# A decoder trunk on one core: first loads by contraction half, transposes between the first products, banks finished in turn, statistics and sums moved later

## The chip, the cores and the metric

The kernel runs on 1 core of one Trainium2 chip. The metric is device time in microseconds (us) of one execution; shorter is better. Every time below is of that core.

## What is computed

A decoder trunk with two layers on 528 tokens (16 learned meta tokens and 512 of the sequence), width 1024, feed-forward width 2816, all in float32:

```python
h = concatenate([meta, x])
for l in range(2):
    h = layer_norm(ALPHA*h + 0.5*swiglu(h, ffn1_wg[l], ffn1_wu[l], ffn1_wd[l]))   # norm 0, norm 3
    mix = short_conv(h) if l == 0 else forgetting_attention(h, k, v, c)
    h = layer_norm(ALPHA*h + mix)                                                 # norm 1, norm 4
    h = layer_norm(ALPHA*h + 0.5*swiglu(h, ffn2_wg[l], ffn2_wu[l], ffn2_wd[l]))   # norm 2, norm 5
    if l == 0:
        k, v, c = shared_kv(h)
return h[:, 16:]
# swiglu(x, wg, wu, wd) = (silu(x @ wg) * (x @ wu)) @ wd
# layer_norm: mean and variance over the 1024 features of each token, then gain and bias
```

The gains, biases and the scalar factor of each norm are as in the reference; the text below speaks of the six norms by the numbers 0 to 5 above.

## The kernel before

Activations lie transposed, features on the partitions and tokens in the columns: `y` is 128 x 8 x 528. The tokens are worked on in two **halves** of 264 columns (256 in layer 1). Every product of two float32 matrices is three matmuls of split operands: a CAST on ScalarE (ACT) gives the high part (`xh`, `wh`), a subtraction on VectorE (DVE) the low part (`xl`, `wl`), and `gemms` (line 244) issues `wl*xh`, `wh*xl`, `wh*xh` for each 128-row slice of the contraction. One such slice of one product is called a **job**. `split_w` (lines 132, 134) splits weights, `split_x` (lines 257, 258) activations. PE's order is the order in which the code is written (a manual schedule); ACT, DVE, the DMA queue of SP and POOL are ordered by a scheduler, which `behind(...)` ties to instructions named to it. `later(n, fn)` calls `fn` after `n` further jobs.

The work is a sequence of stages. In a feed-forward block gate and up products are computed by **units** of 256 columns each of wg and wu. Most units (class `Unit`) use a scheme of seven products p1 to p7 instead of eight, on sums of weight blocks (`Quads.sums`, s1 to s4, lines 200 to 211) and sums of activations (`Mixed.sums`, t1 to t4, lines 326 to 337). The first unit behind a norm (class `Direct`) computes its eight products plainly: half 0, then half 1, each over four PSUM banks (`pc`), first contraction half n=0 for all four, then n=1, then `finish` for both column blocks m (Silu, line 669; product with the up part, line 670; split). Weights come in through `Quads.load` (line 183), one load for each contraction half and matrix.

A norm is spread over the products in front of it. `Norm.add` (lines 409 to 416) sums values and squares as the tiles of `y` are made (line 508). `Norm.post` (line 424) multiplies the sums by a matrix of ones, four matmuls that give mean and mean square of each column; `down` calls it through `later(LAG[h], ...)`, that is 4 jobs behind the last tile of half 0 and 8 jobs behind that of half 1. `Norm.finish` then subtracts (434), forms the inverse root (350 to 358) in a chain on DVE, and for each pair of tiles subtracts and multiplies (444, 445), applies gain and bias on ACT (448) and splits (257, 258). The products of half 0 of the next stage run while half 1 goes through this.

At the very start `x` and `meta` arrive with tokens on the partitions. They are loaded in column halves (lines 706 and 711), transposed by PE (line 729, three transposes for each of eight tiles m and each token half), copied to `y` on ACT (line 733) and split. `turn_x(0)` writes all 24 transposes of half 0 ahead of the first product; the 24 of half 1 stand in one block behind the first 8 jobs.

The last stage, norm 5, transposes back and takes its statistics with `bn_stats` (line 1113), two groups of 512 for each 128 tokens.

Of the kernel before, what the change touches and what calls it, by code (L numbers as in the profile page):

```python
# [9 lines left out]
F32 = mybir.dt.float32  # L10
# [8 lines left out]
P = 128  # L19
# [13 lines left out]
CHUNKS = ((0, 4), (4, 6), (10, 6), (16, 6))  # L33

LEAD = 3
LAG = (4, 8)
SOON = 600
AHEAD = 3

# [7 lines left out]
def trunk_kernel(  # L47
# [59 lines left out]


    newest = []

    @contextmanager
    def behind(*after):
# [7 lines left out]
    def split_w(src, shape, home=None):  # L120

        n = math.prod(shape)
        if home:
            wh, wl = (home(t).rearrange("p k c -> p (k c)")[:, :KD * P] for t in ("wh", "wl"))
        else:
            wh = wp.tile([P, KD * P], F32R, tag="wh", name="wh")
            wl = wp.tile([P, KD * P], F32R, tag="wl", name="wl")
        if len(shape) == 3:
            a, b = (t[:, :n].rearrange("p (j k n) -> p j k n", j=shape[0], k=shape[1]) for t in (wh, wl))
        else:  # L130
            a, b = (t[:, :n].rearrange("p (k n) -> p k n", k=shape[0]) for t in (wh, wl))
        nc.scalar.copy(a, src)  # L132
        with behind(*newest[-1:]):
            nc.vector.tensor_tensor(b, src, a.bitcast(F32), ALU.subtract)  # L134
        return a, b

    class Weights:
# [147 lines left out]
    class Mixed:  # L285
# [26 lines left out]
        def early(self):  # L312
# [2 lines left out]
            self.left("a11")  # L315
            self.left("a12")

        def sums(self):

            b = self.part  # L320
            w = self.w
            new = lambda n: gtile(n, 2 * w).rearrange("p (k c) -> p k c", k=2)
            t = {}
            for k in range(0, KH, 2):
                t1 = new("t1")
                nc.vector.tensor_tensor(t1, b(0, 0, k), b(0, 1, k), ALU.subtract)
                split_x(*self.tiles("t1", k), t1)
            self.left("s1")
            for k in range(0, KH, 2):
                t3, t2 = new("t3"), new("t2")  # L330
                nc.vector.tensor_tensor(t3, b(1, 1, k), b(0, 1, k), ALU.subtract)
                nc.vector.scalar_tensor_tensor(t2, b(0, 0, k), -1.0, t3, ALU.mult, ALU.subtract)
                split_x(*self.tiles("t2", k), t2)
                split_x(*self.tiles("t3", k), t3)
                t[k] = t2
            for k in range(0, KH, 2):
                nc.vector.scalar_tensor_tensor(t[k], t[k], -1.0, b(1, 0, k), ALU.mult, ALU.subtract)
                split_x(*self.tiles("t4", k), t[k])

        def __getitem__(self, name):  # L340
            if name == "b12":
# [242 lines left out]
    class Direct:  # L584
# [6 lines left out]
        def half(self, h, finish):  # L591
            ps = {(j, m): psum(f"pc{j}{m}")[:, :self.w] for m in range(2) for j in range(2)}
            for n in range(2):
                jobs = []
                for m in range(2):
                    wh, wl = self.quads(f"a{m + 1}{n + 1}")
                    jobs += [(ps[j, m], (wh[:, j], wl[:, j]), self.xs[f"b{n + 1}{h + 1}"])
                             for j in range(2)]
                gemms(jobs, range(KH), start=n == 0, stop=n == 1, chained=True)
            for m in range(2):  # L600
                last = finish(m, h, ps[0, m], ps[1, m])
            return last

    def first_four(quads):
# [2 lines left out]
    def run_units(units, finish, direct=None, after=None):  # L607

        if direct:
            xs = units[0].xs
            for h in range(2):
                last = units[0].half(h, direct)
                if h == 0:
                    with behind(*last):
                        xs.sums()
            if after:
                after(0)
        i0 = int(direct is not None)  # L620
        units[i0].p1()
        units[i0].p2()
        for i, u in list(enumerate(units))[i0:]:
            nxt = units[i + 1] if i + 1 < len(units) else None
            u.p5()
            u.p6()
            u.p7()
            if nxt:
                nxt.p1()
            u.p4()  # L630
            u.p3()
            finish(i, u)
            if after:
                after(i)
            if nxt:
                nxt.p2()
# [4 lines left out]
    def ffn(layer, wg, wu, wd, ln, xs, to, last=None, ready=None, ahead=None):  # L641
# [3 lines left out]
        for c, (f0, fn) in enumerate(CHUNKS):  # L645
# [20 lines left out]

            def direct(m, h, pg, pu, split_h=split_h):
                sg = gtile("sg", w)
                nc.scalar.activation(sg, pg, AF.Silu)  # L669
                nc.vector.tensor_tensor(sg, sg, pu, ALU.mult)  # L670
                return split_h(m, h * w, sg)

            units = []
            for i in range(fn // 2):
# [27 lines left out]
    half = D // 2  # L702
    rows = ((0, P), (P, 120), (248, P), (376, P), (504, 8))
    mt = [htile("mt", F32)[:M, :half] for _ in range(2)]
    for j in range(2):
        nc.sync.dma_start(mt[j], meta[:, j * half:(j + 1) * half])
    xt = []
    for i, (r0, n) in enumerate(rows):
        xt.append([htile("xt", F32)[:n, :half] for _ in range(2)])
        for j in range(2):  # L710
            nc.sync.dma_start(xt[-1][j], x[0, r0:r0 + n, j * half:(j + 1) * half])
        if i == 1:
            first.load(0)
    first.load(1)
    vr = gtile("vr", P)[:120]
    nc.gpsimd.dma_start(vr[0:48, :], ln_gain.rearrange("l i (m p) -> (l i m) p", p=P))
    nc.gpsimd.dma_start(vr[48:96, :], ln_bias.rearrange("l i (m p) -> (l i m) p", p=P))
    nc.gpsimd.dma_start(vr[96:120, :], conv_w[0].rearrange("j (m p) -> (j m) p", p=P))
    nc.gpsimd.dma_start(fbias, f_bias.unsqueeze(1))

    def turn_x(h):
        c0, w = SPAN[0][h]
        for m in range(KD):
            ps = psum("pt")
            parts = [(mt, M)] if h == 0 else []
            parts += [(xt[i], rows[i][1]) for i in ((0, 1) if h == 0 else (2, 3, 4))]
            o = 0
            for src, n in parts:
                nc.tensor.transpose(
                    out=ps[:, o:o + n], in_=src[m // KH][:, (m % KH) * P:(m % KH + 1) * P],  # L730
                    identity=ident[:n, :n])
                o += n
            nc.scalar.copy(y[:, m, c0:c0 + w], ps[:, :w])
            if m % 2:
                xs0.made(h, m - 1)
    def turn_vecs():
        ps = psum("pvec")
        nc.tensor.transpose(out=ps[:, :120], in_=vr, identity=ident[:120, :120])
        nc.vector.tensor_copy(vecs, ps[:, :120])

    turn_x(0)
    first_four(first)()
    later(KD, lambda: turn_x(1))
    later(8 * KD, turn_vecs)


# [346 lines left out]
    def last(w, kn, operands):  # L1093

        gain, bias = (
            xtile(n, F32).rearrange("p k c -> p (k c)")[:, :D] for n in ("gain", "bias"))
        nc.gpsimd.dma_start(gain, ln_gain[1, 2:3, :].broadcast_to([P, D]))
        nc.gpsimd.dma_start(bias, ln_bias[1, 2:3, :].broadcast_to([P, D]))
        for h in range(2):
            yv = cols(y, h, 1)  # L1100
            pt = {}
            st = tiny.tile([P, 2, 2, 6], F32, tag="st", name="st")

            def turn(m, yv=yv, pt=pt, st=st):
                g = m // 4
                for t in range(2):
                    if m % 4 == 0:
                        pt[t, g] = psum("pout")
                    nc.tensor.transpose(
                        out=pt[t, g][:, (m % 4) * P:(m % 4 + 1) * P],  # L1110
                        in_=yv[:, m, t * P:(t + 1) * P], identity=ident)
                    if m % 4 == 3:
                        nc.vector.bn_stats(out=st[:, t, g, :], in_=pt[t, g])

            def finish(h=h, pt=pt, st=st):
                mv = tiny.tile([P, 2, 2], F32, tag="mv", name="mv")
                for t in range(2):
                    nc.vector.bn_aggr(out=mv[:, t, :], in_=st[:, t, :, :])
                v, r, a = (tiny.tile([P, 2], F32, tag=n, name=n) for n in "vra")
                nc.vector.tensor_scalar(v, mv[:, :, 1], 4 * EPS, None, ALU.add)  # L1120
                rsqrt(v, r, a)
                for t in range(2):
                    for g in range(2):
                        o = gtile("o", 512)
                        c = slice(g * 512, (g + 1) * 512)
                        nc.vector.scalar_tensor_tensor(
                            o, pt[t, g], mv[:, t, 0:1], gain[:, c], ALU.subtract, ALU.mult)
                        nc.vector.scalar_tensor_tensor(
                            o, o, r[:, t:t + 1], bias[:, c], ALU.mult, ALU.add)
                        r0 = (2 * h + t) * P  # L1130
                        nc.sync.dma_start(out[0, r0:r0 + P, c], o)

            for (m, _), ps in products(
                    [(m, h) for m in range(KD)], w, kn, operands, {}, 1, 0 if h else 3):
                nc.vector.tensor_tensor(yv[:, m, :], yv[:, m, :], ps, ALU.add)
                later(4 + kn * max(0, 3 - m) * h, lambda m=m, turn=turn: turn(m))
            later(KD // 2, finish)
        flush()
# [34 lines left out]
```

## Time and profile before

| | |
|---|---|
| median of 3 runs | 1925.3 us (1923.21 to 1926.7) |
| the profiled execution: its own time | 1922.97 us |
| the profiled execution: span | 1921.2 us |
| mean granted TensorE clock in it | 0.994 |
| PE (matmul) busy | 1878.4 us, 98% of the span |
| DVE busy | 1417.4 us, 74% |
| ACT busy | 875.6 us, 46% |

The profiled execution is 2.3 us below the median. The span runs from the first to the last event that the profiler sees; 1.8 us of the time lie around it. A timeline row gives the start in us from the start of the span, the duration in us, the engine, the line, the operation, out<-in, the shape, and how many like rows were put together; a bracket at its end gives the engine's idle time in front of it and what ended that.

### The profile page before, as it was taken

To read this page: it belongs to the slowest core of one execution; us is meant where nothing else is said; L and a number is where in the kernel's file an instruction comes from. 1 tells how busy PE (TensorE), PEld (TensorE's weight loads), DVE (VectorE), ACT (ScalarE), POOL (GpSimd) and SP (SyncE) were. 2 spreads that over 40 slices of the span, in tenths; PEclk is the share of its full clock that TensorE was granted. 3 is DMA by queue.
4 is the path that set the end of the run, shared out by engine and by line. 5 is a ranking of instruction groups with operands and counts; after the bars stand their busy time and mean duration, and the time that the engine had idled before them with its cause. 6 is when DMAs were issued, how large, how long until landed. Compare 5 with 4: busy or idle time off the path is not lost.

```text
span 1921.2 us, 34484 instructions
## 1 busy us (share of the span) xinstructions
PE 1878.4 (98%) x14467; PEld 1818.5 (95%) x14467; DVE 1417.4 (74%) x2188; ACT 875.6 (46%) x1459; POOL 25.4 (1%) x78
## 2 busy tenths in 40 slices
PE   8999999999999999999999999999999999999997
PEld 7999999999999999999899998989998898989897
DVE  4885858774479776767997887767787787867685
ACT  5353535443245353535454543535455554535360
POOL 0000000000000000000021000000000000000000
PEclk9999999999999999999999999999999999999999
DMA  4333333323330332323224323232523303333241
GB/s 146 100 102 97 101 98 101 98 77 107 103 99 23 121 110 89 110 89 110 88 91 156 111 83 115 83 115 83 182 64 115 99 1 121 98 101 111 90 131 44
DMA packets 180680, 190.41 MB, mean 99 GB/s; under 512 B 5834, under 2 KB 174070, under 8 KB 180526
## 3 DMA queue, kind: packets, MB, share of 16 engines
q1 hardware_dynamic: 178510, 182.74, 29.8%
q0 software_dynamic: 2016, 5.49, 0.8%
q8 instruction: 113, 1.85, 0.4%
q14 instruction: 41, 0.34, 0.1%
HBM read 181.76 MB, written 6.44 MB: 98 GB/s over the span
## 4 chain that ended last, share of the span: by engine, by line
PE 83%; DVE 11%; DMA 3%; ACT 2%; issue 1%; SPq 0%; DVEq 0%; ACTq 0%
PE pb L244 26%; PE pc L244 14%; PE pa L244 6%; PE pcb L244 2%; PE pcv L244 2%; PE pcc L244 2%; PE pq L244 2%; DVE wl L134 2%; DVE xl L258 1%; ACT wh L132 1%; PE psc L977 1%; PE po L1035 1%; DVE y L445 1%; DVE y L508 1%; DVE s L416 1%
## 5 line engine op out<-in xcount | busy, mean ns | idle before, releaser
L132 ACT CAST wh<-raw 128x1024 fp32r<-128x1024 f32 (+1 forms) x440 | 438.6, 1003 | 471.3 <-PE pc L244 73.5
L134 DVE TENSOR_TENSOR wl<-raw,wh 128x1024 fp32r<-128x1024 f32 (+1 forms) x440 | 509.1, 1164 | 189.6 <-ACT wh L132 181.4
L244 PE MATMUL pb<-xh,wl 128*128 128x264 f32 (+1 forms) x1408 | 399.5, 284 | 3.0 <-DVE wl L134 3.0
L244 PE MATMUL pb<-xh,wh 128*128 128x264 f32 (+1 forms) x1408 | 399.7, 284 | 0.0
L244 PE MATMUL pb<-xl,wh 128*128 128x264 f32 (+1 forms) x1408 | 399.3, 284 | 0.0
L244 PE MATMUL pc<-xh,wl 128*128 128x264 f32 (+1 forms) x960 | 275.3, 287 | 6.2 <-ACT sg L669 3.2
L244 PE MATMUL pc<-xl,wh 128*128 128x264 f32 (+1 forms) x960 | 274.4, 286 | 0.5 <-DVE xl L258 0.5
L244 PE MATMUL pc<-xh,wh 128*128 128x264 f32 (+1 forms) x960 | 274.0, 285 | 0.0
L244 PEld LDWEIGHTS pb<-xh,wl 128*128 128x128 f32 x1408 | 265.9, 189 | 3.8 <-issue 3.4
L244 PEld LDWEIGHTS pb<-xh,wh 128*128 128x128 f32 x1408 | 266.0, 189 | 0.0
L244 PEld LDWEIGHTS pb<-xl,wh 128*128 128x128 f32 x1408 | 265.7, 189 | 0.3
L244 PEld LDWEIGHTS pc<-xh,wl 128*128 128x128 f32 x960 | 182.8, 190 | 7.6 <-ACT sg L669 3.7
L244 PEld LDWEIGHTS pc<-xl,wh 128*128 128x128 f32 x960 | 182.8, 190 | 1.0 <-DVE xl L258 0.9
L244 PEld LDWEIGHTS pc<-xh,wh 128*128 128x128 f32 x960 | 183.1, 191 | 0.0
L244 PE MATMUL pa<-xh,wl 128*128 128x264 f32 (+1 forms) x352 | 99.7, 283 | 0.0
L244 PE MATMUL pa<-xh,wh 128*128 128x264 f32 (+1 forms) x352 | 99.7, 283 | 0.0
L244 PE MATMUL pa<-xl,wh 128*128 128x264 f32 (+1 forms) x352 | 99.6, 283 | 0.0
L132 ACT CAST wh<-s 128x1024 fp32r<-128x1024 f32 x44 | 46.1, 1047 | 48.5 <-DVE s L200 12.7
L200 DVE TENSOR_TENSOR s<-raw 128x1024 f32<-128x1024 f32 x44 | 53.7, 1220 | 17.5 <-DMA raw<-in_ffn_wu_dram 16.6
L244 PEld LDWEIGHTS pa<-xh,wh 128*128 128x128 f32 x352 | 66.2, 188 | 0.0
L244 PEld LDWEIGHTS pa<-xh,wl 128*128 128x128 f32 x352 | 66.2, 188 | 0.0
L244 PEld LDWEIGHTS pa<-xl,wh 128*128 128x128 f32 x352 | 66.1, 188 | 0.0
(1920 smaller groups left out, 4458.0 us busy)
## 6 DMA issues: line engine op xcount, KB each, us to landing
raw<-in_ffn_wg_dram SPq DMA_DIRECT2D x88, 512.0 KB, 3.9
raw<-in_ffn_wu_dram SPq DMA_DIRECT2D x88, 512.0 KB, 4.8
raw<-in_ffn_wd_dram SPq DMA_DIRECT2D x48, 768.0 KB, 4.6
raw<-in_conv_w_in_dram SPq DMA_DIRECT2D x12, 1024.0 KB, 4.9
raw<-in_ffn_wd_dram SPq DMA_DIRECT2D x16, 512.0 KB, 3.6
raw<-in_kv_w_dram SPq DMA_DIRECT2D x16, 512.0 KB, 4.8
raw<-in_conv_w_out_dram SPq DMA_DIRECT2D x4, 1024.0 KB, 5.3
raw<-in_attn_w_q_dram SPq DMA_DIRECT2D x4, 1024.0 KB, 4.8
```

Of the source, the lines that this page charges most:

```text
L132: nc.scalar.copy(a, src)
L134: nc.vector.tensor_tensor(b, src, a.bitcast(F32), ALU.subtract)
L200: nc.vector.tensor_tensor(s, a21, a22, ALU.add)
L244: nc.tensor.matmul(ps, lhsT=a[:, k, :], rhs=b(k), start=start and k == ks[0] and j == 0, stop=stop and k == ks[-1] and j == 2, skip_group_ ...
L258: return a, nc.vector.tensor_tensor(dst_l, src32, dst_h.bitcast(F32), ALU.subtract)
L416: self.last[h] = nc.vector.tensor_tensor(self.s2[h], self.s2[h], sq, ALU.add)
L445: nc.vector.tensor_tensor(ym, ym, rb, ALU.mult)
L508: norm.add(h, m, lambda ym=ym, ps=ps: nc.vector.tensor_tensor(ym, ym, ps, ALU.add))
L977: nc.tensor.matmul(ps, lhsT=q[:, M + t * P:M + (t + 1) * P], rhs=kt[:, a:b], start=True, stop=True)
L1035: nc.tensor.matmul(po[:, q0:S], lhsT=vt[:, j * P:(j + 1) * P], rhs=pT[j // 2][:, j % 2, q0:S], start=j == 0, stop=False)
```

## The change

1. SP's queue: the first column halves of `meta` and of the first two blocks of `x`, then the first contraction half of the first weights, then the second halves of each, then the rest of `x`.
2. PE: only the first four tiles' transposes of half 0 stand ahead of the first product; the other four groups come behind jobs 4, 6, 8 and 10, and the eight groups of half 1 behind jobs 12, 14, ... 26.
3. `Direct.half`: in the second contraction half the products run job by job, and `finish(m)` follows each column block's pair of banks.
4. `LAG` goes from (4, 8) to (8, 16) jobs: the four statistics matmuls of norms 0 to 4 come 4 jobs (12 matmuls) later for half 0 and 8 jobs (24 matmuls) later for half 1.
5. `Mixed.sums` is cut in three: t1 as before; t2 and t3 (`more`) ordered behind the Silu of the first column block of half 1; t4 (`fourth`) behind a split of weights.
6. `last`: `bn_stats` on four groups of 256 in place of two of 512 for each 128 tokens.

```diff
-LAG = (4, 8)
+LAG = (8, 16)
...
     class Mixed:
         def sums(self):
             for k in range(0, KH, 2):
                 t1 = self.new("t1")
                 nc.vector.tensor_tensor(t1, b(0, 0, k), b(0, 1, k), ALU.subtract)
                 split_x(*self.tiles("t1", k), t1)
             self.left("s1")
+        def more(self):
             for k in range(0, KH, 2):
...
+        def fourth(self):
+            for k, t in self.t.items():
+                nc.vector.scalar_tensor_tensor(t, t, -1.0, self.part(1, 0, k), ALU.mult, ALU.subtract)
+                split_x(*self.tiles("t4", k), t)
...
     class Direct:
-                gemms(jobs, range(KH), start=n == 0, stop=n == 1, chained=True)
-            for m in range(2):
-                last = finish(m, h, ps[0, m], ps[1, m])
+                if n == 0:
+                    gemms(jobs, range(KH), stop=False, chained=True)
+                    continue
+                for m in range(2):
+                    for job in jobs[2 * m:2 * m + 2]:
+                        gemms([job], range(KH), start=False, chained=True)
+                    last = finish(m, h, ps[0, m], ps[1, m])
...
     def run_units(units, finish, direct=None, after=None):
-            for h in range(2):
-                last = units[0].half(h, direct)
-                if h == 0:
-                    with behind(*last):
-                        xs.sums()
+            with behind(*units[0].half(0, direct)):
+                xs.sums()
+            with behind(units[0].half(1, direct)[0]):
+                xs.more()
...
-            if nxt:
-                nxt.p1()
-            u.p4()
-            u.p3()
+            with behind(*(recent if direct and i == i0 else ())):
+                if direct and i == i0:
+                    xs.fourth()
+                if nxt:
+                    nxt.p1()
+                u.p4()
+                u.p3()
...
             def direct(m, h, pg, pu, split_h=split_h):
-                nc.scalar.activation(sg, pg, AF.Silu)
+                silu = nc.scalar.activation(sg, pg, AF.Silu)
-                return split_h(m, h * w, sg)
+                return silu, *split_h(m, h * w, sg)
...
     for j in range(2):
         nc.sync.dma_start(mt[j], meta[:, j * half:(j + 1) * half])
+        for i in range(2):
+            load_x(i, j)
+        first.load(j)
+    for j in range(2):
+        for i in range(2, 5):
+            load_x(i, j)
...
-    turn_x(0)
+    for m in range(KH):
+        turn_x(0, m)
     first_four(first)()
-    later(KD, lambda: turn_x(1))
+    for h in range(2):
+        for m in range(KH * (1 - h), KD):
+            later(2 * m + 16 * h - 4, lambda h=h, m=m: turn_x(h, m))
...
-                    if m % 4 == 3:
-                        nc.vector.bn_stats(out=st[:, t, g, :], in_=pt[t, g])
+                    if m % 2:
+                        nc.vector.bn_stats(
+                            out=st[:, t, m // 2, :], in_=pt[t, g][:, (m % 4 - 1) * P:(m % 4 + 1) * P])
```

Two places show how it moves instructions. The first is the start of SP's queue (`mt`: meta tokens, `xt`: blocks of `x`, `raw`: weights; the lines are those of each kernel). Before:

```order
L706 DMA mt<-in_meta_dram 16x512 x2
L711 DMA xt<-in_x_dram 128x512 x2
L711 DMA xt<-in_x_dram 120x512 x2
L183 DMA raw<-in_ffn_wg_dram 128x4x256
L183 DMA raw<-in_ffn_wu_dram 128x4x256
L711 DMA xt<-in_x_dram 128x512 x4
```

With the change:

```order
L726 DMA mt<-in_meta_dram 16x512
L723 DMA xt<-in_x_dram 128x512
L723 DMA xt<-in_x_dram 120x512
L184 DMA raw<-in_ffn_wg_dram 128x4x256
L184 DMA raw<-in_ffn_wu_dram 128x4x256
L726 DMA mt<-in_meta_dram 16x512
L723 DMA xt<-in_x_dram 128x512
L723 DMA xt<-in_x_dram 120x512
L184 DMA raw<-in_ffn_wg_dram 128x4x256
L184 DMA raw<-in_ffn_wu_dram 128x4x256
L723 DMA xt<-in_x_dram 128x512 x2
```

The first weights have three loads ahead of them in place of six, and the second contraction half of the weights stands ahead of the last six blocks of `x`.

The second place is ACT's queue at the second half of norm 1, behind the statistics matmuls `pd` (L433 or L441 squares the mean, L448 or L456 applies gain and bias, `xh<-y` is the split's cast, `sg<-pc` the Silu of the first direct unit's half 0 for its two column blocks). Before:

```order
L433 ACTIVATE v<-pd 128x264
L448 ACTIVATE y<-y,vecs 128x264 x3
L257 CAST xh<-y 128x528
L448 ACTIVATE y<-y,vecs 128x264
L669 ACTIVATE sg<-pc_6571 128x264
L257 CAST xh<-y 128x528
L448 ACTIVATE y<-y,vecs 128x264 x3
L257 CAST xh<-y 128x528
L448 ACTIVATE y<-y,vecs 128x264
L257 CAST hh<-sg 128x264
L257 CAST xh<-y 128x528
L669 ACTIVATE sg<-pc_6573 128x264
```

With the change:

```order
L441 ACTIVATE v<-pd 128x264
L683 ACTIVATE sg<-pc_6571 128x264
L683 ACTIVATE sg<-pc_6573 128x264
L456 ACTIVATE y<-y,vecs 128x264 x3
L258 CAST xh<-y 128x528
L456 ACTIVATE y<-y,vecs 128x264 x2
```

Both Silus of half 0 now stand ahead of the first gain-and-bias instruction of half 1; before, the first stood behind four of them and the second behind all eight. At norm 4 the order moves in the same way.

## Rows read from the trace of the kernel before

**Rows 1.** The page, head and busy time.

```profile
span 1921.2 us, 34484 instructions
PE 1878.4 (98%) x14467; PEld 1818.5 (95%) x14467; DVE 1417.4 (74%) x2188; ACT 875.6 (46%) x1459; POOL 25.4 (1%) x78
```

**Rows 2.** Waits of PE: waited for, us in total, times, longest.

```profile
PE pd L424 <- DVE y L508: 9.8, 6, 2.3
```

**Rows 3.** Timeline of PE, from the first transposes to the first products.

```profile
7.25 0.46 PE L729 MATMUL pt<-ident,xt 120*128 120x120 f32 x1 [2.46 <-DMA xt<-in_x_dram]
...
8.46 0.28 PE L729 MATMUL pt<-ident,mt 16*128 16x16 f32 x1
...
9.28 0.28 PE L729 MATMUL pt<-ident,mt 16*128 16x16 f32 x1
...
16.21 0.56 PE L244 MATMUL pc<-xh,wl 128*128 128x264 f32 x1 [2.76 <-DVE wl L134]
...
22.06 2.05 PE L729 MATMUL pt<-ident,xt 128*128 128x128 f32 x11
```

**Rows 4.** Chain of waits, first load of weights.

```profile
3.51 5.62 DMA raw<-in_ffn_wg_dram
```

**Rows 5.** Timeline of ACT and DVE, the first split of weights.

```profile
13.76 1.05 ACT L132 CAST wh<-raw 128x1024 fp32r<-128x1024 f32 x1
14.84 1.23 DVE L134 TENSOR_TENSOR wl<-raw,wh 128x1024 fp32r<-128x1024 f32 x1 [0.53 <-DMA raw<-in_ffn_wg_dram]
```

**Rows 6.** Timeline of PE, holes behind the start.

```profile
56.99 0.36 PE L244 MATMUL pb<-xh,wl 128*128 128x264 f32 x1 [1.14 <-DVE wl L134]
...
74.31 0.39 PE L244 MATMUL pd__783<-hl,wh 128*128 128x264 f32 x1 [0.84 <-DVE hl L258]
...
391.73 0.71 PE L424 MATMUL pd<-y,ones_all 128*128 128x264 f32 x2 [2.25 <-DVE y L508]
...
618.88 0.36 PE L244 MATMUL pb<-xh,wl 128*128 128x264 f32 x1 [1.90 <-DVE wl L134]
...
635.11 0.40 PE L244 MATMUL pd__7119<-hl,wh 128*128 128x264 f32 x1 [0.95 <-DVE hl L258]
...
952.58 0.71 PE L424 MATMUL pd<-y,ones_all 128*128 128x264 f32 x2 [2.19 <-DVE y L508]
...
964.29 0.39 PE L244 MATMUL pc<-xl,wh 128*128 128x264 f32 x1 [0.53 <-DVE xl L258]
...
1404.81 1.22 PE L424 MATMUL pd<-y,ones_all 128*128 128x256 f32 x2 [2.27 <-DVE y L508]
...
1586.15 0.58 PE L244 MATMUL pc<-xh,wl 128*128 128x256 f32 x1 [3.19 <-ACT sg L669]
```

**Rows 7.** Stretches behind four holes: us, busy PE, PEld, DVE, ACT, POOL; PEclk; DMA share; GB/s.

```profile
618.88:623.04 4.16, 4.16 (x21) 4.16 (x22) 3.38 (x4) 0.80 (x2) 0.00 (x0) 0.59 0.56 173
1404.81:1408.20 3.39, 3.39 (x9) 2.76 (x9) 2.44 (x4) 0.78 (x3) 0.00 (x0) 0.52 0.10 21
1586.15:1592.30 6.15, 6.15 (x29) 6.15 (x30) 4.82 (x11) 2.86 (x7) 0.00 (x0) 0.50 0.00 0
392.00:396.00 4.00, 4.00 (x28) 3.74 (x28) 4.00 (x8) 0.52 (x2) 0.00 (x0) 1.00 0.27 81
```

**Rows 8.** Timeline, second half of norm 1: statistics, gain and bias, first split, first product.

```profile
582.48 0.61 PE L424 MATMUL pd<-y,ones_all 128*128 128x264 f32 x2
...
590.02 1.61 ACT L448 ACTIVATE y<-y,vecs 128x264 f32<-128x264 f32 x3 [6.07 <-DVE y L445]
...
592.37 0.70 DVE L258 TENSOR_TENSOR xl<-y,xh 128x528 fp32r<-128x528 f32 x1
...
593.05 0.29 PE L244 MATMUL pc<-xh,wl 128*128 128x264 f32 x1
```

**Rows 9.** Timeline of DVE, first half of norm 0 and the last statistics.

```profile
385.42 0.70 DVE L258 TENSOR_TENSOR xl<-y,xh 128x528 fp32r<-128x528 f32 x1
...
1909.76 1.30 DVE L1113 BATCH_NORM_STATS2 st<-pout 128x6 f32<-128x512 f32 x2 [0.42 <-PE pout L1109]
```

More of the change, by code (lines that the diff above doesn't have):

```diff
@@ L109, in trunk_kernel @@
     newest = []
+    recent = []
     @contextmanager
@@ L131, in split_w @@
             a, b = (t[:, :n].rearrange("p (k n) -> p k n", k=shape[0]) for t in (wh, wl))
-        nc.scalar.copy(a, src)
+        recent[:] = [nc.scalar.copy(a, src)]
         with behind(*newest[-1:]):
-            nc.vector.tensor_tensor(b, src, a.bitcast(F32), ALU.subtract)
+            recent.append(nc.vector.tensor_tensor(b, src, a.bitcast(F32), ALU.subtract))
         return a, b
@@ L316, in early, with new @@
             self.left("a12")
+        def new(self, name):
+            return gtile(name, 2 * self.w).rearrange("p (k c) -> p k c", k=2)
         def sums(self):
             b = self.part
-            w = self.w
-            new = lambda n: gtile(n, 2 * w).rearrange("p (k c) -> p k c", k=2)
-            t = {}
             for k in range(0, KH, 2):
-                t1 = new("t1")
+                t1 = self.new("t1")
                 nc.vector.tensor_tensor(t1, b(0, 0, k), b(0, 1, k), ALU.subtract)
@@ L328, in sums @@
             self.left("s1")
+        def more(self):
+            b = self.part
+            self.t = {}
             for k in range(0, KH, 2):
-                t3, t2 = new("t3"), new("t2")
+                t3, t2 = self.new("t3"), self.new("t2")
                 nc.vector.tensor_tensor(t3, b(1, 1, k), b(0, 1, k), ALU.subtract)
@@ L334, in sums @@
                 split_x(*self.tiles("t3", k), t3)
[L335 to L338, printed above, removed]
+                self.t[k] = t2
+        def fourth(self):
+            for k, t in self.t.items():
+                nc.vector.scalar_tensor_tensor(t, t, -1.0, self.part(1, 0, k), ALU.mult, ALU.subtract)
+                split_x(*self.tiles("t4", k), t)
         def __getitem__(self, name):
@@ L704, in trunk_kernel, with load_x @@
     mt = [htile("mt", F32)[:M, :half] for _ in range(2)]
+    xt = [[htile("xt", F32)[:n, :half] for _ in range(2)] for _, n in rows]
+    def load_x(i, j):
+        r0, n = rows[i]
+        nc.sync.dma_start(xt[i][j], x[0, r0:r0 + n, j * half:(j + 1) * half])
     for j in range(2):
         nc.sync.dma_start(mt[j], meta[:, j * half:(j + 1) * half])
[L707 to L714, printed above, removed]
+        for i in range(2):
[4 more added lines that the diff above has]
+            load_x(i, j)
     vr = gtile("vr", P)[:120]
@@ L719, in trunk_kernel, with turn_x @@
     nc.gpsimd.dma_start(fbias, f_bias.unsqueeze(1))
-    def turn_x(h):
+    def turn_x(h, m):
         c0, w = SPAN[0][h]
[L723 to L735, printed above, removed]
+        ps = psum("pt")
+        parts = [(mt, M)] if h == 0 else []
+        parts += [(xt[i], rows[i][1]) for i in ((0, 1) if h == 0 else (2, 3, 4))]
+        o = 0
+        for src, n in parts:
+            nc.tensor.transpose(
+                out=ps[:, o:o + n], in_=src[m // KH][:, (m % KH) * P:(m % KH + 1) * P],
+                identity=ident[:n, :n])
+            o += n
+        nc.scalar.copy(y[:, m, c0:c0 + w], ps[:, :w])
+        if m % 2:
+            xs0.made(h, m - 1)
     def turn_vecs():
@@ L1101, in last @@
             pt = {}
-            st = tiny.tile([P, 2, 2, 6], F32, tag="st", name="st")
+            st = tiny.tile([P, 2, 4, 6], F32, tag="st", name="st")
             def turn(m, yv=yv, pt=pt, st=st):
@@ L1111, in turn @@
                         in_=yv[:, m, t * P:(t + 1) * P], identity=ident)
-                    if m % 4 == 3:
-                        nc.vector.bn_stats(out=st[:, t, g, :], in_=pt[t, g])
+                    if m % 2:
+                        nc.vector.bn_stats(
+                            out=st[:, t, m // 2, :], in_=pt[t, g][:, (m % 4 - 1) * P:(m % 4 + 1) * P])
             def finish(h=h, pt=pt, st=st):
```

## The prediction

> **What bounds it now.** I read the page's head first: PE is busy 1878.4 us of a span of 1921.2 [rows 1]. The change adds no matmul and removes none, so it can win only the 43 us in which PE stands idle, and the stretches in which it runs at a lower clock. The second view is the list of PE's waits: the statistics matmuls (line 424) wait six times for the last tile, 9.8 us in all [rows 2]; the rest is the start and single holes. The third view, PE's timeline, places these [rows 3, 6]; the fourth, the clock by stretch, shows that behind three holes the granted clock was 0.50 to 0.59, the level of 1.2 GHz [rows 7]. Last I read ACT's and DVE's queues at a norm [rows 8], since the change moves work on those.
>
> **The start.** Before, PE transposes from 7.25, one tile's three in 0.82 us, and its first product starts at 16.21 [rows 3]. Between them stand eight tiles (6.6 us), then ACT's cast of the first weights at 13.76, held in ACT's queue by the copies of those tiles, and DVE's low part from 14.84, 1.23 us [rows 5]. Now four tiles come first (3.3 us less). The first weights were issued at 3.51 and took 5.62 us [rows 4]; with three loads ahead in place of six, some 0.5 MB and three issues less, they land about 1.4 us earlier, and the `x` blocks some 1.3 us earlier (5.9 for 7.25). Transposes then end near 9.2, cast and low part near 11.6, and the first product follows there: 4.6 us sooner. The twelve transposes are not gone. They run between the products and cost 3.3 us at the slow pace of [rows 3], about 1.6 us at full clock. The products from 16.21 to 22.06 took 5.85 us for 24, or 0.24 us each, against a mean of 0.130 over the kernel [rows 1, 3]; I let that slow stretch keep its length. Half 0 of the first unit then ends 2.5 to 3 us sooner. The t4 sums, now behind a weight split, no longer delay the low part that p6 waits for: 1.14 us, and 0.84 us at the first down product goes too, as its activations are ready with time to spare [rows 6]. Together **5.2 us**, with bounds of 1 (all moved transposes at the slow pace, loads no earlier) and 7.
>
> The transposes at 7.25 to 13.5 did not bring the products behind them to full speed: these began slow all the same [rows 3]. The Trainium skill, page "TensorE: Matmul & The Clock Gate", section "Part 4: PE-mode transpose", says that transposes do not count as PE work for the clock as matmuls do. This speaks against mixing them with the first products: if the clock rose later by their 3.3 us, half of that, 1.65 us, would be lost, and the start would be worth 3.6 us.
>
> **Norm 0.** In half 0 the statistics come 12 matmuls later. Its waits go, but the next products then wait for the first split, which ended at 386.12 [rows 9] when PE came to them some 0.3 us later: 0.4 us is all that is won. In half 1 the hole of 2.25 [rows 6] goes, with 24 matmuls (24 x 0.12 = 2.9 us) in it, and the second half's split stays ready in time, as the conv's products of half 0 are many. Together **2.7**, bounds 0.4 and 4.
>
> **Norm 1.** Before, statistics at 582.48, ACT's first gain and bias at 590.02, first split finished at 593.07, and PE comes to half 1 at 593.05 [rows 8]: no slack. Now the statistics stand 2.9 us later, and both Silus stand ahead of the gain and bias. The second Silu can start only when PE has ended half 0, at about 593.1. It takes about 0.36 us; from the first gain and bias to the end of the split are 3.05 us (590.02 to 593.07). So the split ends at 596.4: **a new hole of 3.3 us**. Against it the hole of 1.90 at 618.88 goes, since t4 is out of the way of the weight split, with the slow stretch behind it (21 matmuls in 4.16 us, 0.198 each, 1.4 us more than at the mean), and the 0.95 us at 635.11 [rows 6, 7]. What is queued behind the Silus on ACT is the gain and bias of all eight tiles, and for these DVE's splits and PE wait. Net **+0.9**.
>
> **Norm 2.** The 2.19 and 0.53 us [rows 6] go, but the second half's first split ended at 964.2, and with the same DVE work ahead of it it stays there: the two holes become one of about 3.5 us in front of half 1. Only the 0.3 to 0.4 us of half 0 is won: **+0.4**.
>
> **Norm 3.** The 2.27 us go, and the slow stretch (3.39 us at a clock of 0.52, 1.6 us) [rows 6, 7]. Five heads' products cover the chain nearly; I take 1.1 us of new wait and 0.2 in half 0: **+2.6**.
>
> **Norm 4.** As norm 1, a new hole of 3.3 us ahead of half 1. The hole of 3.19 us at 1586.15 [rows 6], where PE waited for a bank that the Silu of half 1 had to free, goes, since that Silu now stands ahead of the sums; with it the slow stretch: 29 matmuls in 6.15 us, 0.212 each, 2.4 us over the mean [rows 7]. Net **+2.3**.
>
> **The end.** DVE's last two statistics groups took 1.30 us [rows 9]; half of each is now done earlier: **+0.5**.
>
> **New slow stretches.** The three new holes (norms 1, 2, 4) are as long as or longer than any in the middle before. Behind 3.19, 1.90 and 2.27 us the clock fell, behind 2.25 us it did not [rows 6, 7]. The cost of such a stretch, from the three that there are, is 2.4, 1.4 and 1.6 us, mean 1.8; bounds for all three together 0 and 7.2 (three at 2.4). I take three at 1.8: **-5.4**.
>
> **The sum:** 5.2 + 2.7 + 0.9 + 0.4 + 2.6 + 2.3 + 0.5 = 14.6, less 5.4: 9.2 us. From the profiled execution's 1922.97 us that is 1913.8. That execution lies 2.3 us below the median of the runs; by the median, 1925.3, I forecast **1916.1 us**.
>
> **Rivals.**
> - *No slow stretch behind the new holes*: 1916.1 - 5.4 = 1910.7. For it: the hole of 2.25 us without one. Against: the longest hole had the longest. Chance 0.2.
> - *The start gives nothing, and the holes are deep*: loads interleave and the first weights land as before, so that only 1 us is won (4.2 less), and the slow stretches cost 2.4 each (1.8 less): 1922.1, within the bound of no change. For it: the two loads of weights and the tail of `x` share the same engines. Against: half the bytes stand ahead of them. Chance 0.12.
> - *The first clock rise comes late* by the transposes among the products: 1.65 us, 1917.8. It was worked out above; by that rule of the Trainium skill it would be so. Chance 0.15; it stays near the forecast.
> - *Later statistics starve PE at all five norms*: the place is PE between half 0 and half 1, the price per norm a hole of 3.3 us and 2.4 us of slow clock, 5.7. It decides if the products left behind the statistics of half 1 are shorter than the chain of 10.6 us from statistics to first split (582.48 to 593.07 [rows 8]). Norms 0 and 3 then lose 5.7 each where I took 0.3 and 1.1 (10 more), and ACT, held by Silus behind that, keeps the holes at 618.88, 635.11 and 1586.15 with their slow stretches (6.0 + 3.8 = 9.8 more): 1936. Against it: at norms 0 and 3 more products lie there than at the others. Chance 0.06.
> - *The change does nothing to the waits* (the scheduler gives back the old order) is excluded by the order above.
>
> **The numbers.** The forecast as worked out has 0.47, no slow stretch 0.2, late rise 0.15, start and holes 0.12, starved 0.06. The range leaves out the starved case and the upper part of the third: 1908.5 (no slow stretch, start at 7) to 1922. About 0.2%, 3.9 us, is what a measurement of this kernel can tell from no change: faster is below 1921.4, slower above 1929.2. All of the first three cases but a small part of each are faster: 0.8; same 0.14; slower 0.06.
>
> **What would show it.** In the profile after: first product near 11.6; no wait of line 424's matmuls for `y`; no hole near 618 and 1586; the start's first 36 down products done near 69 for 74; new holes of PE in front of the second half behind norms 1, 2 and 4, of 3.3, 3.5 and 3.3 us, with a clock of about 0.5 behind each; none of more than 1.5 us at norms 0 and 3. It is wrong if the first product starts later than 14, if PE's idle time does not fall by some 5 us, or if slow stretches stand at other places.

## The result, and the profile after

The changed kernel takes 1913.2 us (median of 4 runs, 1912.77 to 1913.92) for 1925.3 before: a ratio of 0.9938, 95% interval 0.9921 to 0.9956. The forecast was 1916.1, range 1908.5 to 1922.0. The time lies 2.9 us from the forecast, but the parts behind it do not lie where the sum put them. Every ratio is to the kernel before, run again beside the run in question; its medians there were 1926.0 (e1 to e4), 1927.5 (e5 to e7) and 1924.7 us (e8 to e11), so times of different sets are best compared by ratio.

The head of the page after, as in [rows 1]:

```profile
span 1911.7 us, 34484 instructions
PE 1874.8 (98%) x14467; PEld 1814.6 (95%) x14467; DVE 1416.8 (74%) x2196; ACT 877.1 (46%) x1459; POOL 25.4 (1%) x78
```

The span fell by 9.5 us: 3.6 us are busy time of the same 14467 matmuls (less of it at the low clock), 5.9 us are idle time of PE. The waits of PE after, the largest (waited for, us in all, times, longest); those of line 424, 9.8 us in [rows 2], stand no longer among them:

```profile
PE pc L245 <- ACT xh L258: 6.0, 3, 2.2
PE pc L245 <- DVE wl L135: 5.4, 1, 5.4
...
PE pc L245 <- DVE xl L259: 2.1, 4, 0.5
PE pd__7119 L245 <- ACT hh L258: 1.8, 1, 1.8
```

A hole is a stretch in which PE stands idle, a slow stretch one in which its granted clock is 0.50. The three holes for `xh` are new. PE's timeline shows where they stand, as forecast in front of half 1 behind norms 1, 2 and 4, each with a second small one for `xl`, and a further wait at 631, for the split activations `hh` of the down product:

```profile
591.74 0.39 PE L245 MATMUL pc<-xh,wl 128*128 128x264 f32 x1 [2.04 <-ACT xh L258]
592.67 0.39 PE L245 MATMUL pc<-xl,wh 128*128 128x264 f32 x1 [0.54 <-DVE xl L259]
...
631.03 0.39 PE L245 MATMUL pd__7119<-hh,wl 128*128 128x264 f32 x1 [1.78 <-ACT hh L258]
...
960.51 0.39 PE L245 MATMUL pc<-xh,wl 128*128 128x264 f32 x1 [1.84 <-ACT xh L258]
...
1561.09 0.39 PE L245 MATMUL pc<-xh,wl 128*128 128x256 f32 x1 [2.16 <-ACT xh L258]
```

The holes at 391, 618 and 1586 of [rows 6] are gone. The clock behind the four places (columns as in [rows 7]):

```profile
592.00:596.00 4.00, 3.46 (x28) 3.33 (x28) 3.30 (x6) 4.00 (x9) 0.00 (x0) 1.00 0.02 4
631.00:635.00 4.00, 3.61 (x17) 3.41 (x18) 3.28 (x6) 1.47 (x2) 0.00 (x0) 0.64 1.05 353
961.00:965.00 4.00, 3.57 (x29) 3.57 (x30) 3.61 (x7) 4.00 (x9) 0.00 (x0) 1.00 0.01 4
1562.00:1566.00 4.00, 4.00 (x34) 4.00 (x35) 3.16 (x6) 3.68 (x9) 0.00 (x0) 1.00 0.00 0
```

Behind none of the three new holes did the clock fall in this execution; it fell behind the wait at 631, to a mean of 0.64.

To see where time comes from I set the start of each down stage in one trace against the same one before. The lead gained from stage to stage, in us, for the change and all runs told of below (start: up to the last down stage ahead of norm 0; norm 0 and norm 3: up to the output product behind that norm; norms 1, 2 and 4: up to a down stage of the feed-forward block behind that norm, the second for norm 1 and the first for the others; end: from there to the end of the span; the cells hold to about 0.1 us):

| run | start | norm 0 | norm 1 | norm 2 | norm 3 | norm 4 | end | span won |
|---|---|---|---|---|---|---|---|---|
| the change | 0.7 | 2.7 | -1.8 | 1.2 | 3.8 | 3.6 | -0.7 | 9.5 |
| forecast, slow stretches included | 5.2 | 2.7 | -0.9 | -1.4 | 2.6 | 0.5 | 0.5 | 9.2 |
| e9_change_again | 1.3 | 2.2 | -3.4 | -0.3 | 3.8 | 2.0 | -0.7 | 4.8 |
| e1_lag_back | 1.8 | -1.7 | 4.4 | 0.2 | 0.2 | 5.8 | -0.7 | 10.0 |
| e2_start_back | 0.7 | 2.1 | -1.6 | 1.2 | 3.6 | 3.5 | -0.7 | 8.8 |
| e3_bn_back | 0.7 | 2.3 | -1.7 | -0.9 | 3.8 | 2.2 | -0.1 | 6.3 |
| e11_bn_back_again | 1.5 | 2.5 | -1.9 | -0.5 | 1.5 | 2.0 | -0.1 | 5.1 |
| e4_sums_back | -3.1 | 2.5 | -1.2 | 1.0 | 3.1 | -0.7 | -0.5 | 1.0 |
| e10_sums_alone | 1.1 | 0.4 | 5.1 | -1.6 | 0.7 | 5.7 | -0.2 | 11.2 |
| e6_loads_held | 2.5 | 2.4 | -2.7 | 1.2 | 3.9 | 3.8 | -0.7 | 10.4 |
| e7_transposes_first | -0.1 | 2.4 | -2.1 | -0.6 | 3.6 | 2.1 | -0.6 | 4.8 |
| e5_lag_by_norm | 3.4 | 1.9 | 4.4 | -0.4 | 1.9 | 5.7 | -0.8 | 16.0 |
| e8_best | 2.2 | 2.6 | 3.8 | 1.1 | 3.8 | 5.7 | -0.1 | 19.1 |

### The profile page after: what moved, and what is told of

The parts are those of the page before. It is cut to its first block, busy times and chain, and to the rows that moved or that the text cites. A ratio compares the mean times of both kernels' runs of the same rounds, so it can differ in the third digit from the quotient of the medians.

```text
span 1911.7 us, 34484 instructions
## 1 busy us (share of the span) xinstructions
PE 1874.8 (98%) x14467; PEld 1814.6 (95%) x14467; DVE 1416.8 (74%) x2196; ACT 877.1 (46%) x1459; POOL 25.4 (1%) x78
## 4 chain that ended last, share of the span: by engine, by line
PE 88%; DVE 8%; DMA 2%; ACT 1%; issue 1%; SPq 0%; DVEq 0%; ACTq 0%
PE pb L245 26%; PE pc L245 15%; PE pa L245 6%; PE pcc L245 2%; PE pcv L245 2%; PE pcb L245 2%; PE pq L245 2%; DVE wl L135 1%; PE psc L998 1%; PE po L1056 1%; DVE xl L259 1%; ACT wh L133 1%; DMA raw<-in_attn_w_q_dram 1%; DVE y L453 1%; DVE y L452 1%
## 5 line engine op out<-in xcount | busy, mean ns | idle before, releaser
L245 PE MATMUL pc<-xh,wl 128*128 128x264 f32 (+1 forms) x960 | 275.4, 287 | 11.5 <-ACT xh L258 6.0
```

The costliest lines, as they stand in the source:

```text
L245: nc.tensor.matmul(ps, lhsT=a[:, k, :], rhs=b(k), start=start and k == ks[0] and j == 0, stop=stop and k == ks[-1] and j == 2, skip_group_ ...
```

## The experiments

**One part undone: the places of the statistics.**

```diff
-LAG = (8, 16)
+LAG = (4, 8)
```

> The changed kernel with LAG at (4, 8) again, all else of the change kept. Theory (the later statistics are worth their waits at norms 0, 2 and 3 and cost a hole at norms 1 and 4): the waits of the statistics matmuls for y come back, some 9 us of them, and the holes of 2.6 us in front of half 1 at norms 1 and 4 go; together 2 to 4 us slower than the changed kernel's 1913.2, so 1915 to 1917. Rival (the gain of 9.5 us in the profile comes from the sums and the direct unit's order): no change, 1912 to 1914. Rival of the prediction (the later statistics starve PE): faster by over 2 us.

Measured: 1912.6 us (1909.9 to 1914.1), ratio 0.9930 (0.9915 to 0.9945), as fast as the change: the total is that of the first rival. The theory is right about the places and wrong about the sum. Norms 0, 2 and 3 lose 4.4, 1.0 and 3.6 us against the change, and norms 1 and 4 win 6.2 and 2.2: -9.0 and +8.4. Some of both is chance: a slow stretch followed the returned waits at 391 and 1401, and the one at 632 stayed away. So `LAG` as a whole is worth nothing that these runs can tell, by two effects of about the same size.

**One part undone: the start.** The loads and the transposes of the kernel before, in the changed kernel (the "-" side of the change at SP's queue and at `turn_x`, not all of it printed above).

> The changed kernel with the loads in their old order and the transposes in their old blocks. Theory (the first weights land no earlier, as the loads run side by side, and the transposes among the products eat the earlier first product): the end of the first unit moves by under 0.5 us, and the time by under 1 us: 1912 to 1914.2. The prediction's term (the start is worth 2.5 to 3 us up to the end of the first unit's half 0): 1915.7 or more.

Measured: 1914.3 us (1913.3 to 1918.8), start 0.7 as with the change: theory, 0.1 us above its range. The first product came at 16.67 us instead of 13.46, and the first unit still ended 0.2 us sooner (the first `pb` product at 47.01 for 47.24).

**One part undone: the statistics of the end.**

```diff
-            st = tiny.tile([P, 2, 4, 6], F32, tag="st", name="st")
+            st = tiny.tile([P, 2, 2, 6], F32, tag="st", name="st")
...
-                    if m % 2:
-                        nc.vector.bn_stats(
-                            out=st[:, t, m // 2, :], in_=pt[t, g][:, (m % 4 - 1) * P:(m % 4 + 1) * P])
+                    if m % 4 == 3:
+                        nc.vector.bn_stats(out=st[:, t, g, :], in_=pt[t, g])
```

> The changed kernel with bn_stats on two groups of 512. Theory (the finer groups make PE's transposes wait for DVE at the first four tiles of the second half, 1.1 us, and save 0.5 us at the end): 0.6 us faster, 1912.6, and no wait of pout for st. Prediction's term (0.5 us saved): 0.5 us slower, 1913.7.

Measured: 1917.0 us (1915.6 to 1918.8), neither of the two. The end itself behaved as the theory said, -0.1 for -0.7 us, and the wait of `pout` (the bank that PE transposes into at the end) for `st` (its statistics) is gone. But up to norm 1 the traces run alike, and then norms 2 and 4 lost 2.1 and 1.3 us, at places that this edit does not touch: the granted clock was 0.50 in the middle of slow stretches at 964 and 1564. This called for the repeats further down.

**One part undone: the direct unit's order and the cut sums.** `Direct.half`, `Mixed.sums` and `run_units` as before, the rest as changed.

> The changed kernel with the direct unit's banks finished together and the sums in one piece, as before; loads, transposes, LAG and bn_stats as changed. Theory (the holes at the first unit's p6 and at the Silu of the second half go by this part alone, and at norm 1 what is won is given back at the down product): at norm 4 the hole of 3.2 us and its slow stretch come back (5 us or more), at norm 1 the hole near 618 comes back and the wait of 1.8 us near 631 goes, the p6 wait of the first stage (1.1 us) comes back: 1917 to 1921. Rival (LAG moves the Silus and so removes the holes): under 2 us slower.

Measured: 1924.0 us (1917.5 to 1926.9, 10 runs), ratio 0.9992 (0.9980 to 1.0004): without this part nothing is left of the gain; that is 3 us above the theory's range. The start alone lost 3.8 us against the change, with a slow stretch behind the first hole below (0.50 from 58.85), which is chance again. The holes for `wl` are back. The one at the Silu of half 1 is not, against the theory; in its place there are now holes on either side of it:

```profile
57.84 0.36 PE L245 MATMUL pb<-xh,wl 128*128 128x264 f32 x1 [1.79 <-DVE wl L135]
...
621.41 0.36 PE L245 MATMUL pb<-xh,wl 128*128 128x264 f32 x1 [1.38 <-DVE wl L135]
...
1567.06 0.38 PE L245 MATMUL pc<-xl,wh 128*128 128x256 f32 x1 [1.42 <-DVE xl L259]
...
1593.34 0.36 PE L245 MATMUL pb<-xh,wl 128*128 128x256 f32 x1 [1.50 <-DVE wl L135]
```

(In the code `more` stands behind the Silu of the second column block of half 1, `half(1, direct)[0]` being what the last `finish` returns; item 5 of the change names the first.)

**The same part alone, on the kernel before.**

> The kernel before with the direct unit's order and the cut sums alone; loads, transposes, LAG and bn_stats as before. Theory (this part carries nearly all of the gain: the holes at p6 of the first stage, near 618 and near 1586 with their slow stretches, and the Silus out of the way): 9 to 13 us faster than before, 1912 to 1917. Rival (it needs the later statistics to work): under 5 us faster.

Measured: 1911.8 us (1909.9 to 1913.4), ratio 0.9929 (0.9915 to 0.9944): theory. Together with e4 this is the main finding: this part alone gives all that the whole change gives. It wins 5.1 us at norm 1 and 5.7 at norm 4: the holes of 1.90, 0.95 and 3.19 us [rows 6] are gone, and no new one stands in front of half 1 but 0.57 us for `xl` at 1560.69. How much the order of finish wins, and how much the cut sums, was not tried apart. The waits for `y` stay as they were, and cost a slow stretch by chance (0.56 from 946 to 950):

```profile
PE pd L432 <- DVE y L516: 9.8, 6, 2.3
```

**The place of the statistics by norm.**

```diff
-                    later(LAG[h], lambda h=h: norm.post(h))
+                    later((4, 8)[h] if norm.i in (1, 4) else LAG[h], lambda h=h: norm.post(h))
```

> The changed kernel with LAG (4, 8) at norms 1 and 4 and (8, 16) at norms 0, 2 and 3. Theory (at norms 1 and 4 no statistics matmul waited before, so the later place gives nothing there and costs the hole in front of half 1): the two holes of 2.6 us go; at norm 4 that is kept, at norm 1 a part of it may be lost again at the down product, whose weights come no sooner: 2.5 to 5 us faster than the changed kernel, 1908 to 1910.7. Rival (the earlier statistics bring back the late Silu or another hole of the same length): 1912 to 1914.

Measured: 1906.8 us (1905.8 to 1908.7), ratio 0.9894 (0.9875 to 0.9913): theory, 1.2 us below its range. The start gave 2.7 us more than with the change, which this edit does not touch; norms 1 and 4, which it does, gave 6.2 and 2.1 more. Both holes for `xh` at norms 1 and 4 are gone, and the wait at 631 too (0.75 us for `hl` is left). How that wait had come is seen in DVE's queue at the end of the first `Unit` behind norm 1. In the change the low part of the down weights stands ahead of the gate's product L678, and waits for a cast that waits for its load:

```profile
627.39 1.05 ACT L133 CAST wh<-raw 128x1024 fp32r<-128x1024 f32 x1 [1.63 <-DMA raw<-in_ffn_wd_dram]
...
628.47 1.23 DVE L135 TENSOR_TENSOR wl<-raw,wh 128x1024 fp32r<-128x1024 f32 x1 [1.66 <-ACT wh L133]
629.62 0.70 DVE L678 TENSOR_TENSOR g<-g,u 128x528 f32<-128x528 f32 x1
```

With the earlier statistics at this norm the scheduler put them the other way round:

```profile
621.75 0.70 DVE L678 TENSOR_TENSOR g<-g,u 128x528 f32<-128x528 f32 x1
623.41 1.23 DVE L135 TENSOR_TENSOR wl<-raw,wh 128x1024 fp32r<-128x1024 f32 x1 [0.96 <-ACT wh L133]
```

e1 and e10, with the earlier statistics too, have no wait for `hh` there either. That this order, and not the later PE, makes the wait was not tried by itself.

**The first weights without company.** A one-column copy into each later tile makes its load wait (excerpt):

```diff
+            for t in (mt[1], xt[0][1], xt[1][1], *(xt[i][j] for j in range(2) for i in range(2, 5))):
+                held.append(nc.vector.tensor_copy(t[:, 0:1], y[:t.shape[0], 0, 0:1]))
```

> The changed kernel with a one-column copy by DVE into each tile of the second lot of loads, so that these are issued only when the first tile of y is there (near 5.7 us); 10 tiny copies are added, whose columns the loads overwrite. Theory (the first weights landed at 11.1 as before because the later loads share the engines with them): they land at 8 to 9, the first product starts 2 to 3 us sooner than 13.46, and the end is 1.5 to 3 us sooner, 1910.2 to 1911.7. Rival (512 KB loads take their 8 us from issue whatever runs beside them): first product at 13.4, no change. Second rival (the later loads now hold up the second contraction half): first product sooner, but the wait comes back behind the first 16 jobs.

Measured: 1914.3 us (1912.3 to 1918.4), no change. The later loads were issued from 6.14 us on instead of 3.15, and the first weights still landed at 11.0, where ACT's cast begins:

```profile
11.00 1.04 ACT L133 CAST wh<-raw 128x1024 fp32r<-128x1024 f32 x1 [2.60 <-DMA raw<-in_ffn_wu_dram]
...
13.35 0.59 PE L250 MATMUL pc<-xh,wl 128*128 128x264 f32 x1 [5.37 <-DVE wl L135]
17.34 0.28 PE L250 MATMUL pc<-xl,wh 128*128 128x264 f32 x1
```

So 3 us less of company did not bring them sooner, and the theory that the later loads hold them up is not borne out; between 6.14 and 11.0 they still ran beside them. What sets the landing is open; in runs with the same code as the change the landing lay between 9.74 (e5) and 11.10. Start 2.5 comes from elsewhere: full speed was reached 4.0 us after the first product instead of about 8.

**All transposes of half 0 in front.**

```diff
-    for m in range(KH):
+    for m in range(KD):
         turn_x(0, m)
```

> The changed kernel with all 24 transposes of half 0 ahead of the first product; the 24 of half 1 stay between the products. Theory (the weights bind the first product, so eight tiles fit in front of them for nothing, and the products then pass the slow stretch without transposes in between): first product at 13.5 to 13.9, full speed after 24 products, some 2 us sooner than at 21.1, end 1.5 to 2.5 us faster, 1910.7 to 1911.7. Rival (ACT's copies of the four added tiles delay the weight splits by 2 to 3 us, as before): no change or slower.

Measured: 1920.4 us (1916.4 to 1921.3), ratio 0.9961 (0.9945 to 0.9977): the rival, no gain. First product at 17.65, since the copies of the four added tiles wait for `x` (PE stood 1.32, 0.93 and 0.80 us for its parts) and stand ahead of the weight casts on ACT. But the start lost only 0.8 us against the change's first trace and 1.4 against its repeat; 3.3 us more of the difference to the first trace lie at norms 2 and 4, where slow stretches came as they do in the repeat without this edit. So the transposes are better off among the products by about 1 us in these traces, and the rest of the 7 us between the medians is not shown to come from this edit.

**The change itself again.**

> The changed kernel itself, once more, on the chip that runs the others of this set. Theory (whether a slow stretch follows a hole of 2 us is a matter of the execution and not of the program): the holes and waits stand where they stood to 0.3 us, but the slow stretches, and the first rise of the clock, may stand elsewhere; median 1911 to 1918. Rival (the slow stretches belong to the program): the one slow stretch at 632 and the rise near 21.1 as before, median 1912.7 to 1914.

Measured: 1916.2 us (1913.4 to 1918.2), ratio 0.9948 (0.9931 to 0.9965): theory. The holes stand where they stood (2.04, 2.07, 1.86 and 2.16 us at 591.68, 632.65, 962.13 and 1564.23), but now a slow stretch follows every one of them:

```profile
592.00:596.00 4.00, 3.46 (x17) 3.39 (x17) 3.27 (x6) 4.00 (x10) 0.00 (x0) 0.57 0.00 0
633.00:637.00 4.00, 3.64 (x18) 3.61 (x18) 3.10 (x6) 1.28 (x2) 0.00 (x0) 0.57 0.99 345
963.00:967.00 4.00, 3.94 (x22) 3.94 (x23) 3.62 (x7) 4.00 (x11) 0.00 (x0) 0.67 0.03 6
1564.50:1568.50 4.00, 3.51 (x17) 3.39 (x17) 3.21 (x6) 4.00 (x10) 0.00 (x0) 0.58 0.00 0
```

In the four microseconds from 592 PE did 17 matmuls where it did 28 in the first trace. The same program has one slow stretch in one execution and four in another, and spans of 1911.7 and 1916.4 us. Norms 1, 2 and 4 differ between the two by 1.6, 1.5 and 1.6 us: that is about a slow stretch's price here.

**The old statistics of the end again.**

> e3_bn_back once more, beside the changed kernel on the same chip. Theory (its 1917.0 came from slow stretches by chance behind the holes of norms 2 and 4, not from bn_stats): within 3 us of e9_change_again on either side, and in the profile 0.5 us less than it between the last down products and the end. Rival (bn_stats on two groups is slower by 3 to 4 us): 3 to 4 us over e9_change_again again, with the slow stretches at norms 2 and 4.

Measured: 1915.0 us (1914.8 to 1917.9), 1.2 us under the change beside it: theory. The end took 0.1 us more than before, with the change 0.7 more, in both pairs of traces. At norm 3 this trace gained 1.5 us where the change gained 3.8: PE waited 1.51 us for `first` at 1371.32 and 0.77 us for `wl` at 1382.49, waits that the change's two traces do not have; e5 has the like (1.16 and 0.77). Why was not looked into.

**The parts that win, together** (e5 and e3's edits).

> LAG (4, 8) at norms 1 and 4, (8, 16) at norms 0, 2 and 3, and bn_stats on two groups of 512; all else as changed. Theory (the two parts add up: no hole in front of half 1 at norms 1 and 4, no wait of pout for st): 0.5 us under e5_lag_by_norm's 1906.8, so 1904 to 1909 with slow stretches that come or stay away by chance; no wait of pout for st in the profile. Rival (bn_back as a whole costs 3 us, as e3_bn_back's 1917.0 against 1913.2 would have it): 1909.5 or more.

Measured: 1904.7 us (1903.8 to 1905.9), ratio 0.9894 (0.9879 to 0.9908): in the theory's range. This beats both kernels: 20 us faster than before beside it, 8.5 to 11.5 faster than the change. By ratio it is no faster than e5, so what the old statistics of the end add shows in the stage alone (-0.1 for -0.8). No slow stretch was seen in its trace ahead of the last down stage's end.

## Why the prediction held, and where it did not

The time was in the range and near the forecast because errors of both signs met: the start, norm 1 and the end gave 6.6 us less than forecast, norms 2, 3 and 4 gave 6.9 more. That they cancel is luck. One part of the mechanism was right throughout: the terms that the prediction gives to the cut sums and the order of finish (1.14 and 0.84 at the start, 1.90, 1.4 and 0.95 at norm 1, 3.19 and 2.4 at norm 4, the slow stretches of before among them) make 11.8 us, and e10, which has this part alone, won 11.9 at these three places. By its own steps:

- *The start, 5.2 us.* Measured 0.7 in the profile and 1.3 in the repeat: the step that failed. Its own parts add up to 4.5 to 5.0 and not to 5.2. Two of its terms were wrong. The first is "they land about 1.4 us earlier". It goes by the load of `wg` alone, which landed at 9.13 [rows 4]; the split takes columns of `wg` and `wu`, and `wu` came later. Before, it was issued at 3.95 and took 7.2 us:

```profile
L183 SPq DMA_DIRECT2D raw<-in_ffn_wu_dram x1: 507/507/507, 4.0 to 4.0; - x1
...
DMA to landing us min/median/max: 7.2/7.2/7.2
```

  With the change it was issued at 2.60 and took 8.42 us (row of the chain of waits), and released ACT's cast:

```profile
2.60 8.42 DMA raw<-in_ffn_wu_dram
...
11.10 1.04 ACT L133 CAST wh<-raw 128x1024 fp32r<-128x1024 f32 x1 [2.66 <-DMA raw<-in_ffn_wu_dram]
```

  So the weights were there at 11.0 for 11.2, and the first product came at 13.46 and not at 11.6. (This trace is the latest of the eight with the new start, e6 and e7 left out: that cast began at 9.74 to 11.10, mean 10.5.) The second is "I let that slow stretch keep its length": it grew from 5.85 to about 7.7 us (13.46 to 21.1), with the transposes in it:

```profile
13.46 0.59 PE L245 MATMUL pc<-xh,wl 128*128 128x264 f32 x1 [5.44 <-DVE wl L135]
...
20.79 0.42 PE L245 MATMUL pc<-xh,wh 128*128 128x264 f32 x1
21.14 0.23 PE L746 MATMUL pt<-ident,mt 16*128 16x16 f32 x1
...
21.83 0.28 PE L245 MATMUL pc<-xh,wh 128*128 128x264 f32 x1
```

  This is the mechanism of the rival of the late rise, in this trace at about half the size given there: 24 products ran at the low clock before and 24 now, with two groups of transposes among them and a third at the rise. The Trainium skill's page "TensorE: Matmul & The Clock Gate", section "Part 4: PE-mode transpose", would have it so, and this pair of traces agrees. The other traces do not settle it: with the same code the slow stretch lasted 4.05 us in e5, where the first full-speed product is at 16.14 and the first product at 12.09, and 6.2 us in e1. Over those eight traces the first unit ended at 44.18 to 47.24, mean 46.3; over the three with the old one at 46.66 to 47.01, mean 46.85. So the loads and the transposes are worth some 0.5 us by these means, with 3 us of chance, where 2.5 to 3 were forecast. The holes at p6 and at the first down product (1.14 and 0.84 us) went or shrank as said, by the cut sums: in e4 they are back, in e10 they are not.
- *Norm 0, 2.7 us.* Measured 2.7; and it goes when `LAG` goes back.
- *Norm 1, 0.9 less a slow stretch.* The new hole was forecast at 3.3 (its own terms make 3.4) and is 2.6 us in two pieces. The holes at 618 and its slow stretch went as said. But "the 0.95 us at 635.11" did not go: it became 1.78 and 0.35 us, and there the slow stretch came. Net -1.8 for a forecast of -0.9: sign right, cause half missed.
- *Norm 2, 0.4 less a slow stretch.* Measured 1.2: the first split came about 1.2 us sooner than I let it, so the one hole is 1.84 and 0.54 us and not 3.5 (which is not worked out there: the terms beside it make 3.1).
- *Norm 3, 2.6.* Measured 3.8: the new wait is 0.5 us and not 1.1; the slow stretch at 1404 went too.
- *Norm 4, 2.3 less a slow stretch.* Measured 3.6, the hole 2.65 in two pieces for 3.3, and no slow stretch this time.
- *The end, 0.5 us won.* Measured 0.7 lost, and 0.5 to 0.8 in all traces with the finer groups, for 0.1 to 0.2 without. DVE's last statistics did shrink from the 1.30 us of [rows 9] to 0.76. But PE's transposes of the first four tiles now wait for DVE's statistics of the bank that they write to, and more is given away there than is won at the end: 0.6 us at the second half, whose rows these are, and 0.5 at the first (near 1869). With two groups (e3, e8) neither place loses:

```profile
1891.26 0.88 PE L1130 MATMUL pout<-ident,y 128*128 128x128 f32 x4 [0.44 <-DVE st L1134]
...
1900.77 0.76 DVE L1134 BATCH_NORM_STATS2 st<-pout 128x6 f32<-128x256 f32 x2 [0.42 <-PE pout L1130]
```

- *The slow stretches, 5.4 us.* None of the three came in the profiled execution, all three in the repeat. The mean price of 1.8 us was about right (1.5 to 1.6 measured); that it is certain was wrong. The rows of before could have told: the prediction names one hole of about 2 us without a slow stretch, at 391, but behind the 2.19 us at 952 [rows 6] the clock stayed up too (columns as in [rows 7]):

```profile
952.58:956.60 4.02, 4.02 (x26) 3.76 (x27) 4.02 (x7) 0.79 (x3) 0.00 (x0) 1.00 0.00 0
```

  *The rival of no slow stretch* (1910.7, chance 0.2) describes the first trace at norms 1, 2 and 4 better than the forecast does.
- *The rival of starved norms* fell: norms 0 and 3 have holes of 1.3 and 0.5 us. But its mechanism is there on a smaller scale, at norms 1 and 4, and costs all that the later statistics win at the others.
- *The range and the signs.* The lower end by its own terms is 1910.7 - 1.8 = 1908.9 and not 1908.5. Of the signs, the waits of the statistics matmuls for `y` and the holes near 618 and 1586 went, and PE's idle time fell by 5.9 us; the first 36 down products were done at 72.6 and not near 69. One sign of being wrong came true: the slow stretch of the profiled execution stood at 632, where none was forecast.

## What to carry to other kernels

A constant that moves one step in five places should be read at each of them: where a wait stood in front of the step, moving it later wins that wait, and where none stood, it only shortens the cover of the chain behind it. Here one number for all five norms came out at about zero, and the old number put back at two of them won 8.3 us at those two stages (e5). When a time agrees with a sum, compare the terms stage by stage before believing the sum; and undo the parts one by one, since here one of the four parts that were undone carried the gain.

## What the runs showed of the hardware that was not expected

The same program, with holes equal to 0.3 us, had a slow stretch of TensorE behind one of four holes in one execution and behind all four in another; 1.9 us of hole at 618 [rows 6, 7] was followed by one, and 2.25 us at 391 and 2.19 at 952 were not. At the start the first full-speed product came 4.0 to 10.4 us behind the first product (e6, and e9 with 12.51 and 22.91). On this kernel that makes spans of one program differ by 5 us, as much as most single edits here are worth, so that such edits are better judged by their stage in the trace than by the total.
